# Down projection of a two-layer decoder trunk: weight combinations, residuals and sums of squares all on VectorE, second weight tile in a tile of its own

## The chip, the cores and the metric

One core of one Trainium2 chip runs the whole kernel in one launch. The metric is the device time of the launch in microseconds (us); lower is better. The kernel before takes 2494.03 us (median of 3 runs, 2493.29 to 2494.21).

## What is computed

Two decoder layers on 1024 positions of width 1024, in fp32: a mixer, a SwiGLU feed-forward block and a gated embedding per layer. The change lies in the last product of the feed-forward block, in both layers.

```python
def swiglu(h, w_gate, w_up, w_down):
    return (jax.nn.silu(h @ w_gate) * (h @ w_up)) @ w_down
...
h = h + swiglu(rmsnorm(h, g_ffn[layer]), w_gate[layer], w_up[layer], w_down[layer])
gate = jax.nn.sigmoid(rmsnorm(h, g_ple[layer]) @ w_ple_gate[layer])
h = h + gate * (p[layer] @ w_ple_proj[layer])
```

`w_down` is 2816 x 1024 per layer.

## The kernel before

An fp32 operand is split into a rounded high part and a low rest (`split`, line 145: ScalarE casts the high part, L146, VectorE subtracts it, L147), and each 128x512 product takes three matmuls (`mm3`, lines 189 to 191).

`ffn_down` (line 653) computes the product with `w_down` by Winograd's form of Strassen's scheme on 2x2 blocks: seven products j, in the order 1, 2, 5, 6, 3, 7, 4, instead of eight. Each product has 11 **steps** f = 0 to 10, one per 128 rows of half of `w_down`; step s = 0 to 76 counts through all seven. A step needs one weight tile (128x512) and one activation tile `ra` (128x512, written to DRAM earlier by `ffn_up`), and gives 4 PSUM tiles x 3 = 12 matmuls, 924 in all for a layer. I call the 11 steps of one j a **block**.

The weight tile of a step is made by `left` (line 667). For j = 1, 2, 4 it is a quarter of `w_down` as it is. For the others it is a combination, one add or subtract of 128x512: L673 (j = 5, two tiles read, the sum goes to a kept tile `sd`, one for each f), L677 (j = 6, from `sd` and one tile read), L681 (j = 3, likewise), L684 (j = 7, two tiles read). In the kernel before `tt` (line 659) puts all four on GpSimd (POOL in the profile). Every tile read is a `raw` tile (profile name `rd`), of which there are 6 (`RAW`); so a step of j = 5 or 7 takes two of them.

`run` (line 746) goes through the steps: matmuls of step s, then `prepare(s + 7)`, which reads and combines the weight tile and splits both operands of a step seven ahead. The split tiles are 8 deep. In step f = 8 of a block `before(j)` reads four tiles of the residual and adds the kept partial results `u` or `v` to them (`residual`, L702, POOL). At the end of a block `after(j, ps)` empties the four PSUM tiles: ScalarE copies (j = 1, 5), or VectorE adds (L723), and for j = 6 four adds `v = v + u` on POOL (L733). PSUM tiles come from 6 banks, a block uses 4, so a block's third tile (c = 2) takes the bank that the previous block's first tile (c = 0) held: **matmuls of c = 2 in a block's first step wait for the first add of `after`**. `done` (line 705) scales a finished tile for the next product (L150, L151) and adds its square to a sum `S` (`stat`, L259: POOL, the last of each half on VectorE).

All reads and writes go through one queue, SP. Each engine works through its own queue in order; the framework's scheduler fixes that order when the kernel is built, and it moves instructions ahead of where the source has them. The residual stream's tiles are `hm` (read, line 406) and `hf` (written, line 708).

Of the kernel before, what the change touches and what calls it, by code (L numbers as in the profile page):

```python
# [11 lines left out]
F32 = mybir.dt.float32  # L12
# [4 lines left out]
ALU = mybir.AluOpType  # L17
# [4 lines left out]
P = 128  # L22
T = 1024
D = 1024
KT = D // P
NT = T // P
HT = 512
# [12 lines left out]
RAW = 6  # L40
# [6 lines left out]
class Build:  # L47
# [198 lines left out]
            )  # L246
        return y

    def stat(self, st, n, i, last, src):

        nc = self.nc
        if i == 0:
            st[n] = self.tp.tile([P, HT], F32, tag="S", name=self.name("S"), bufs=2)
            nc.scalar.activation(st[n], src, AF.Square)
        else:
            sq = self.tmp("sq")
            nc.scalar.activation(sq, src, AF.Square)  # L257
            eng = nc.vector if i == last else nc.gpsimd
            eng.tensor_tensor(out=st[n], in0=st[n], in1=sq, op=ALU.add)  # L259

    def tok_scale(self, S, dim, r):
# [63 lines left out]
def trunk(ctx, tc, x, p, positions, g_mix, g_ffn, g_ple, ev_w_in, ev_w_conv, ev_g_v, ev_w_s,  # L325
          ev_b_s, ev_w_out, od_w_in, od_b_gate, od_g_qa, od_g_kva, od_w_q_up, od_w_kv_up, od_g_q,
          od_g_k, od_g_mh, od_w_out, w_gate, w_up, w_down, w_ple_proj, w_ple_gate, out):
    nc = tc.nc
    B = Build(tc)
    x = x[0]  # L330
    out = out[0]
# [316 lines left out]
    half = NFF // 2  # L648
# [4 lines left out]
    def ffn_down(l, act_d, h_d, h2_d, X2, st, normed):  # L653

        steps = [(j, f) for j in (1, 2, 5, 6, 3, 7, 4) for f in range(half)]
        ready, chain, u, v, res = {}, {}, {}, {}, {}
        tt = nc.gpsimd.tensor_tensor

        def part(fh, ch, f):
            t = B.wp.tile([P, HT], F32, tag="raw", name=B.name("rd"), bufs=RAW)
            r = (fh * half + f) * P
            nc.sync.dma_start(t, w_down[l][r : r + P, ch * HT : (ch + 1) * HT])
            return t

        def left(j, f):
            if j in (1, 2, 4):
                return part(j != 1, j == 4, f)
            if j == 5:  # L670
                a, b = part(0, 1, f), part(1, 1, f)
                c = chain[f] = B.slot(32 + f if f < 8 else 35 + f, F32, "sd")
                tt(out=c, in0=a, in1=b, op=ALU.add)  # L673
                return c
            if j == 6:
                a, c = part(0, 0, f), chain[f]
                tt(out=c, in0=c, in1=a, op=ALU.subtract)  # L677
                return c
            if j == 3:
                a = part(1, 0, f)  # L680
                tt(out=a, in0=a, in1=chain[f], op=ALU.subtract)  # L681
                return a
            a, b = part(0, 0, f), part(0, 1, f)
            tt(out=a, in0=a, in1=b, op=ALU.subtract)  # L684
            return a

        def prepare(s):
            j, f = steps[s]
            b = B.slot(RA_SLOTS[s % len(RA_SLOTS)], F32, "ra")
            nc.sync.dma_start(b, act_d[j][f])  # L690
            a = left(j, f)
            wh = B.wp.tile([P, HT], F32R, tag="whi", name=B.name("hd"), bufs=8)
            wl = B.wp.tile([P, HT], F32R, tag="wlo", name=B.name("ld"), bufs=8)
            B.split(wh, wl, a)
            bs = B.slots2(2 * (s % 8), 2 * (s % 8) + 1, "act")
            B.split(bs[0], bs[1], b)
            ready[s] = (wh, wl), bs

        def residual(n, k, plus):
            t = load(h_d[n][k], "res")  # L700
            if plus is not None:
                tt(out=t, in0=t, in1=plus, op=ALU.add)  # L702
            return t

        def done(n, k, t):
            make_ple(l, X2, n, k, t)
            B.stat(st, n, k, KT - 1, t)
            nc.sync.dma_start(h2_d[n][k], t)

        def before(j):  # L710

            for c in range(4):
                if j == 2:
                    res[c] = residual(1, c, u[c])
                elif j == 3:
                    res[c] = residual(0, c, v[c])
                elif j == 7:
                    res[c] = residual(0, c + 4, v[c])
                elif j == 4:
                    res[c] = residual(1, c + 4, u[c])  # L720

        def after(j, ps):
            add = lambda o, a, b: nc.vector.tensor_tensor(out=o, in0=a, in1=b, op=ALU.add)  # L723
            for c in range(4):
                if j == 1:
                    u[c] = B.slot(46 + c, F32, "ud")
                    nc.scalar.copy(u[c], ps[c])
                elif j == 5:
                    v[c] = B.slot(50 + c, F32, "vd")
                    nc.scalar.copy(v[c], ps[c])  # L730
                elif j == 6:
                    add(u[c], ps[c], u[c])
                    tt(out=v[c], in0=v[c], in1=u[c], op=ALU.add)  # L733
                else:
                    if j == 7:
                        add(u[c], ps[c], u[c])
                    add(res[c], ps[c], res[c])
                    n, k = {2: (1, c), 3: (0, c), 7: (0, c + 4), 4: (1, c + 4)}[j]
                    if j == 4:
                        done(n, k, res[c])  # L740
                    else:
                        B.later(c + 1, lambda n=n, k=k, t=res[c]: done(n, k, t))
            if j == 7:
                B.later(4, lambda: normed(0))

        def run():
            for s, (j, f) in enumerate(steps):
                if f == 0:
                    ps = [B.ps("pd") for _ in range(4)]
                if f == half - 3:  # L750
                    before(j)
                a, b = ready.pop(s)
                for c in range(4):
                    w = slice(c * P, (c + 1) * P)
                    B.mm3(ps[c], (a[0][:, w], a[1][:, w]), b, f == 0, f == half - 1)
                B.tick()
                if s + AHEAD < len(steps):
                    prepare(s + AHEAD)
                if f == half - 1:
                    after(j, ps)  # L760
                if s == len(steps) - 4:
                    tok = load_p(l, 0)
            return tok

        return prepare, run
# [187 lines left out]
    for hq in range(2):  # L953
        t = B.tp.tile([P, 4, P], F32, tag="S", name=B.name("wsr"), bufs=2)
        nc.sync.dma_start(t, ev_w_s[0, hq * 4 : hq * 4 + 4].rearrange("h t s -> t h s"))
        nc.gpsimd.affine_select(
            out=t, in_=t, pattern=[[0, 4], [-1, P]], compare_op=ALU.is_ge, fill=0.0, base=0,
# [68 lines left out]
    for pr in range(4):  # L1026
        u = u_unit(pr) if pr else u0
# [12 lines left out]
    for ch in range(4):  # L1040
# [3 lines left out]
        u = B.w_unit(w_in[:, 512 + ch * P : 512 + (ch + 1) * P], KT, P, f"c{ch}", G_MIX)  # L1044
        for n in range(2):
            pc = B.ps(f"pc{ch}")
            B.ws_mm(pc, u, KT, X[n])
            c = B.tmp("cs")
# [3 lines left out]
        u = B.w_unit(w_in[:, 1024 + ch * P : 1024 + (ch + 1) * P], KT, P, f"x{ch}", G_MIX)  # L1052
        ys = []
        for n in range(2):
# [8 lines left out]
            for i in (1, 0):  # L1063
                nc.vector.scalar_tensor_tensor(
                    out=y, in0=z[n][:, i : i + HT], scalar=w[i], in1=y, op0=ALU.mult, op1=ALU.add
# [3 lines left out]
        u = B.w_unit(w_in[:, ch * P : (ch + 1) * P], KT, P, f"b{ch}", G_MIX)  # L1069
# [123 lines left out]
    for i in range(16):  # L1193
# [3 lines left out]
        out=ang, in0=posf.unsqueeze(2).to_broadcast([P, NT, 16]),  # L1197
        in1=freq.unsqueeze(1).to_broadcast([P, NT, 16]), op=ALU.mult,
# [3 lines left out]
        out=turns, in0=ang, scalar1=1.0 / (2 * math.pi), scalar2=ROUND, op0=ALU.mult, op1=ALU.add  # L1202
    )
    nc.vector.tensor_scalar(
        out=turns, in0=turns, scalar1=-ROUND, scalar2=None, op0=ALU.add
    )
    fl = lambda t: t.rearrange("p a b -> p (a b)")
    for c in (TWO_PI_A, TWO_PI_B, TWO_PI_C):
        nc.vector.scalar_tensor_tensor(
            out=fl(ang), in0=fl(turns), scalar=-c, in1=fl(ang), op0=ALU.mult, op1=ALU.add  # L1210
        )
    nc.vector.tensor_scalar(
        out=ang, in0=ang, scalar1=3.1415925, scalar2=-3.1415925, op0=ALU.min, op1=ALU.max
# [5 lines left out]
        out=fl(ang), in0=fl(ang), scalar=-1.0, in1=fl(ang), op0=ALU.mult, op1=ALU.max  # L1219
    )  # L1220
    nc.vector.tensor_scalar(
        out=ang, in0=ang, scalar1=-1.0, scalar2=math.pi / 2, op0=ALU.mult, op1=ALU.add
# [10 lines left out]
        out=qsc[0:NOPE, :], in0=vec[0:NOPE, G_Q : G_Q + 1], scalar1=sc, scalar2=None, op0=ALU.mult  # L1233
# [200 lines left out]
    for tt in range(NT):  # L1434
# [3 lines left out]
        for c in range(2):  # L1438
# [6 lines left out]
            out=q[:, :, 0:NOPE], in0=q[:, :, 0:NOPE],  # L1445
            in1=rn.unsqueeze(2).to_broadcast([P, H, NOPE]), op=ALU.mult,
# [3 lines left out]
            out=qp, in0=q[:, :, NOPE:QK], in1=rp.unsqueeze(2).to_broadcast([P, H, RP]), op=ALU.mult  # L1450
        )
        nc.gpsimd.tensor_tensor(
            out=qp, in0=qp, in1=gqp.unsqueeze(1).to_broadcast([P, H, RP]), op=ALU.mult
# [3 lines left out]
        t = B.tmp("mv")  # L1457
# [23 lines left out]
    for tt in range(NT):  # L1481
# [3 lines left out]
        k = zp.tile([P, H, QK], F32, tag="q", name=B.name("k"), bufs=2)  # L1485
        v = B.tmp("v", (P, H, DV))
        rt = rkv[tt // 4][:, tt % 4 : tt % 4 + 1]
        for c in range(2):
# [10 lines left out]
            out=k[:, :, 0:NOPE], in0=k[:, :, 0:NOPE],  # L1499
            in1=rn.unsqueeze(2).to_broadcast([P, H, NOPE]), op=ALU.mult,  # L1500
# [3 lines left out]
        t = B.tmp("mo")  # L1504
# [25 lines left out]
    for n in range(2):  # L1530
        t = mq_part(0, n, B.ps("mq"))
# [29 lines left out]
    def load_V(pr):  # L1561
# [14 lines left out]
        out=mf, in_=mf, pattern=[[-1, P]], compare_op=ALU.is_ge, fill=NEG, base=0,  # L1576
# [7 lines left out]
        out=mf, in_=mf, pattern=[[1, P]], compare_op=ALU.is_ge, fill=NEG, base=0,  # L1584
# [260 lines left out]
    for i, u in enumerate(units):  # L1845
        h, b = u
# [93 lines left out]
```

## Time and profile before

| | us |
|---|---|
| median of 3 runs | 2494.03 |
| the profiled execution | 2495.41 |
| its span, first to last instruction | 2493.7 |
| TensorE busy (PE) | 2428.1, 97% of the span |
| VectorE busy (DVE) | 1574.7, 63% |
| GpSimd busy (POOL) | 991.7, 40% |
| ScalarE busy (ACT) | 988.2, 40% |
| down stage of layer 0 / of layer 1 (first to last `pd` matmul) | 795.5 to 1015.7 / 2146.7 to 2365.5 |

The profiled execution is 1.7 us longer than its span and 1.4 us longer than the median. In the rows below PE, DVE, ACT and POOL are the four engines that compute, SPq is the queue of reads and writes. Names such as `rd` or `pd` are the program's tiles, with numbers left out; `pd` are the PSUM tiles of the down stage. In square brackets behind an instruction stands how long its engine was idle before it, and what ended that.

### The profile page before, as it was taken

What the parts mean: (1) busy time and instruction counts of PE and PEld (TensorE: products, weight loads), DVE (VectorE), ACT (ScalarE), POOL (GpSimd) and SP (SyncE); (2) the same over time, 40 slices, a digit from 0 to 9 for tenths busy, and PEclk for the clock granted to TensorE, in tenths of its full rate; (3) what the DMA queues carried; (4) which work ended last, traced back from release to release, by engine and by line L of the source; (5) the groups of instructions that cost most, each with busy time, mean ns of one, the idle gap of its engine ahead of it and who ended that gap; (6) DMA issues with size and microseconds to landing.
All of it is one profiled execution on the core that took longest, in us unless ns stands there. A gap on an engine that the chain in (4) does not pass through costs nothing. (4 is left out here: it accounts for less than half of the span.)

```text
span 2493.7 us, 34019 instructions
## 1 busy us (share of the span) xinstructions
PE 2428.1 (97%) x11510; PEld 2004.3 (80%) x11510; DVE 1574.7 (63%) x2879; ACT 988.2 (40%) x1877; POOL 991.7 (40%) x878
## 2 busy tenths in 40 slices
PE   8999998999999998999999999999999999999999
PEld 6878886788888887788888788877788888887877
DVE  6863477545456798776785566557755554697832
ACT  5321344233233545444554455534333232454520
POOL 3452125746553564212321132113556556275400
PEclk9999999999999999999999999999999999999999
DMA  4221443433236857553454843154433233786821
GB/s 149 81 81 51 144 152 96 141 97 110 93 105 208 274 187 258 168 177 95 115 152 124 212 114 104 49 165 123 123 123 114 89 106 106 249 266 192 295 101 39
DMA packets 358686, 350.75 MB, mean 141 GB/s; under 512 B 24011, under 2 KB 249648, under 8 KB 358512
## 3 DMA queue, kind: packets, MB, share of 16 engines
q1 hardware_dynamic: 358016, 348.25, 44.6%
q8 instruction: 90, 1.47, 0.2%
q0 software_dynamic: 464, 0.33, 0.1%
q14 instruction: 84, 0.69, 0.1%
q10 hardware_dynamic: 32, 0.01, 0.0%
HBM read 255.18 MB, written 93.32 MB: 140 GB/s over the span
## 5 line engine op out<-in xcount | busy, mean ns | idle before, releaser
L189 PE MATMUL pd<-acth,hd 128*128 128x512 f32 x616 | 241.9, 393 | 12.3 <-DVE res L723 12.3
L190 PE MATMUL pd<-actl,hd 128*128 128x512 f32 x616 | 241.1, 391 | 0.0
L191 PE MATMUL pd<-acth,ld 128*128 128x512 f32 x616 | 240.9, 391 | 0.0
L259 POOL TENSOR_TENSOR S<-S,sq 128x512 f32<-128x512 f32 x62 | 89.4, 1441 | 255.7 <-ACT sq L257 254.9
L189 PE MATMUL p<-xch,hg 128*128 128x512 f32 x440 | 175.2, 398 | 10.8 <-ACT o L548 8.7
L191 PE MATMUL p<-xch,lg 128*128 128x512 f32 x440 | 174.3, 396 | 0.0
L190 PE MATMUL p<-xcl,hg 128*128 128x512 f32 x440 | 173.9, 395 | 0.0
L189 PE MATMUL p<-xch,hu 128*128 128x512 f32 x440 | 172.9, 393 | 0.0
L191 PE MATMUL p<-xch,lu 128*128 128x512 f32 x440 | 172.9, 393 | 0.0
L190 PE MATMUL p<-xcl,hu 128*128 128x512 f32 x440 | 172.6, 392 | 0.0
L147 DVE TENSOR_TENSOR actl<-ra,acth 128x512 fp32r<-128x512 f32 x154 | 165.2, 1075 | 11.3 <-ACT acth L146 11.1
L189 PEld LDWEIGHTS pd<-acth,hd 128*128 128x128 f32 x616 | 116.6, 189 | 37.5 <-DVE res L723 13.2
L146 ACT CAST hu<-ru 128x512 fp32r<-128x512 f32 x116 | 71.6, 622 | 188.0 <-PE p L190 175.2
L190 PEld LDWEIGHTS pd<-actl,hd 128*128 128x128 f32 x616 | 116.6, 189 | 24.2
L191 PEld LDWEIGHTS pd<-acth,ld 128*128 128x128 f32 x616 | 116.5, 189 | 24.4
L147 DVE TENSOR_TENSOR ld<-rd,hd 128x512 fp32r<-128x512 f32 x110 | 101.6, 923 | 51.3 <-ACT hd L146 51.0
L146 ACT CAST hg<-rg 128x512 fp32r<-128x512 f32 x110 | 68.2, 620 | 158.0 <-PE p L190 131.7
L540 POOL TENSOR_TENSOR act<-act,sg 128x512 f32<-128x512 f32 x60 | 88.6, 1479 | 103.0 <-DVE act L533 102.9
L147 DVE TENSOR_TENSOR lu<-ru,hu 128x512 fp32r<-128x512 f32 x116 | 118.8, 1024 | 15.0 <-ACT hu L146 15.0
L146 ACT CAST hd<-rd 128x512 fp32r<-128x512 f32 x110 | 68.3, 621 | 140.8 <-PE pd L190 61.6
L189 PEld LDWEIGHTS p<-xch,hg 128*128 128x128 f32 x440 | 83.5, 190 | 32.7 <-ACT o L548 9.5
L146 ACT CAST acth<-ra 128x512 fp32r<-128x512 f32 x154 | 94.7, 616 | 26.9 <-DMA ra<-act 22.2
(553 smaller groups left out, 6825.7 us busy)
## 6 DMA issues: line engine op xcount, KB each, us to landing
rd<-in_w_down SPq DMA_DIRECT2D x198, 256.0 KB, 4.1
ra<-act SPq DMA_DIRECT2D x154, 256.0 KB, 3.9
rg<-in_w_gate SPq DMA_DIRECT2D x100, 256.0 KB, 3.3
ru<-in_w_up SPq DMA_DIRECT2D x100, 256.0 KB, 2.9
act<-act SPq DMA_DIRECT2D x88, 256.0 KB, 2.0
act<-at SPq DMA_DIRECT2D x66, 256.0 KB, 2.0
rpg<-in_w_ple_gate SPq DMA_DIRECT2D x48, 256.0 KB, 3.0
rwo<-in_ev_w_out SPq DMA_DIRECT2D x32, 256.0 KB, 2.8
```

The lines of the kernel that those rows point to most:

```text
L146: self.nc.scalar.copy(hi, src)
L147: (eng or self.nc.vector).tensor_tensor(out=lo, in0=src, in1=hi.bitcast(F32), op=ALU.subtract)
L189: mm(ps, a[0], b[0], start=first, stop=False, skip_group_check=more)
L190: mm(ps, a[0], b[1], start=False, stop=False, skip_group_check=more)
L191: mm(ps, a[1], b[0], start=False, stop=last, skip_group_check=more)
L259: eng.tensor_tensor(out=st[n], in0=st[n], in1=sq, op=ALU.add)
L540: (nc.vector if last else nc.gpsimd).tensor_tensor(out=t, in0=t, in1=sg[d["i"], key], op=ALU.mult)
```

## The change

- `tt` becomes VectorE: the 44 combinations of a stage (L673, L677, L681, L684), the 16 residual adds (L702) and the 4 adds `v = v + u` (L733).
- `done` passes VectorE to `stat`: the 12 adds of squares of a stage that POOL had (L259).
- For j = 5 and j = 7 the second weight tile is read straight into the `sd` tile of that f, not into a `raw` tile. For j = 5 the combination is then made in place.
- The four residual tiles of a block are no longer read and added together in step 8, but one each in steps 5, 6, 8 and 9.

```diff
-    def stat(self, st, n, i, last, src):
+    def stat(self, st, n, i, last, src, eng=None):
...
-            eng = nc.vector if i == last else nc.gpsimd
+            eng = eng or (nc.vector if i == last else nc.gpsimd)
             eng.tensor_tensor(out=st[n], in0=st[n], in1=sq, op=ALU.add)
...
-        tt = nc.gpsimd.tensor_tensor
-
-        def part(fh, ch, f):
-            t = B.wp.tile([P, HT], F32, tag="raw", name=B.name("rd"), bufs=RAW)
+        tt = nc.vector.tensor_tensor
+
+        def part(fh, ch, f, t=None):
+            if t is None:
+                t = B.wp.tile([P, HT], F32, tag="raw", name=B.name("rd"), bufs=RAW)
...
+            spot = lambda: B.slot(32 + f if f < 8 else 35 + f, F32, "sd")
             if j == 5:
-                a, b = part(0, 1, f), part(1, 1, f)
-                c = chain[f] = B.slot(32 + f if f < 8 else 35 + f, F32, "sd")
-                tt(out=c, in0=a, in1=b, op=ALU.add)
+                a, c = part(0, 1, f), part(1, 1, f, spot())
+                chain[f] = c
+                tt(out=c, in0=a, in1=c, op=ALU.add)
                 return c
...
-            a, b = part(0, 0, f), part(0, 1, f)
+            a, b = part(0, 0, f), part(0, 1, f, spot())
             tt(out=a, in0=a, in1=b, op=ALU.subtract)
             return a
...
-            B.stat(st, n, k, KT - 1, t)
+            B.stat(st, n, k, KT - 1, t, nc.vector)
...
-                if f == half - 3:
-                    before(j)
+                if f in (5, 6, 8, 9):
+                    before(j, (5, 6, 8, 9).index(f))
```

The number of instructions and of transfers stays the same. VectorE's queue grows by 152 instructions (76 a stage) and POOL's shrinks by as many. What that does to the queues is seen at two places of layer 0; the numbers behind the names tell tiles apart.

The first place is VectorE's queue just ahead of the four adds that empty the PSUM tiles of product 3. Before, `ld` and `actl` are the low parts of the weight and the activation tile, two rows for a step:

```order
L147 TENSOR_TENSOR ld_8289<-rd_8283,hd_8288 128x512
L147 TENSOR_TENSOR actl_8293<-ra_8281,acth_8292 128x512
L147 TENSOR_TENSOR ld_8316<-rd_8310,hd_8315 128x512
L147 TENSOR_TENSOR actl_8320<-ra_8308,acth_8319 128x512
L723 TENSOR_TENSOR res_8230<-pd_8018,res_8230 128x512
L723 TENSOR_TENSOR res_8233<-pd_8019,res_8233 128x512
```

The same place in the changed kernel (L686 is the old L684, L724 the old L723):

```order
L147 TENSOR_TENSOR ld_8218<-rd_8212,hd_8217 128x512
L147 TENSOR_TENSOR actl_8222<-ra_8210,acth_8221 128x512
L686 TENSOR_TENSOR rd_8376<-rd_8376,sd_8378 128x512
L147 TENSOR_TENSOR ld_8248<-rd_8242,hd_8247 128x512
L147 TENSOR_TENSOR actl_8252<-ra_8240,acth_8251 128x512
L686 TENSOR_TENSOR rd_8411<-rd_8411,sd_8413 128x512
L147 TENSOR_TENSOR ld_8278<-rd_8272,hd_8277 128x512
L147 TENSOR_TENSOR actl_8282<-ra_8270,acth_8281 128x512
L686 TENSOR_TENSOR rd_8446<-rd_8446,sd_8448 128x512
L147 TENSOR_TENSOR ld_8305<-rd_8299,hd_8304 128x512
L147 TENSOR_TENSOR actl_8309<-ra_8297,acth_8308 128x512
L724 TENSOR_TENSOR res_8138<-pd_8007,res_8138 128x512
```

The combinations of product 7 now stand in VectorE's own queue ahead of those adds, four steps ahead of the `ld` of the same step (`rd_8376`, f = 8, stands ahead of `ld_8248`, f = 4).

The second place is the SP queue where it reads product 7's weights. Before, each step has two reads into `raw` tiles beside its `ra`:

```order
L664 DMA rd_8256<-in_w_down 128x512
L690 DMA ra_8281<-act_3164 128x512
L664 DMA rd_8258<-in_w_down 128x512
L664 DMA rd_8283<-in_w_down 128x512
L690 DMA ra_8308<-act_3165 128x512
L664 DMA rd_8285<-in_w_down 128x512
L664 DMA rd_8310<-in_w_down 128x512
```

In the changed kernel it has one there:

```order
L665 DMA rd_8341<-in_w_down 128x512
L692 DMA ra_8339<-act_3166 128x512
L665 DMA rd_8376<-in_w_down 128x512
L692 DMA ra_8374<-act_3167 128x512
L665 DMA rd_8411<-in_w_down 128x512
L692 DMA ra_8409<-act_3168 128x512
L665 DMA rd_8446<-in_w_down 128x512
```

The other half of product 7's weights, the `sd` tiles, is read some 15 steps earlier for f = 0 to 5 (beside the `ra` of products 6 and 3):

```order
L665 DMA sd_8127<-in_w_down 128x512
L692 DMA ra_7761<-act_3156 128x512
L665 DMA sd_8157<-in_w_down 128x512
L665 DMA sd_8187<-in_w_down 128x512
L665 DMA sd_8214<-in_w_down 128x512
L692 DMA ra_7786<-act_3157 128x512
L665 DMA sd_8244<-in_w_down 128x512
```

So the reads of product 7 are spread over a longer stretch of the queue, and half of them no longer wait for a `raw` tile.

## Rows read from the trace of the kernel before

**Rows 1.** The page's section 1: busy us and share of the span, instructions.
```profile
PE 2428.1 (97%) x11510; PEld 2004.3 (80%) x11510; DVE 1574.7 (63%) x2879; ACT 988.2 (40%) x1877; POOL 991.7 (40%) x878
```

**Rows 2.** Waits of PE, whole span: engine, line, releaser: us in total, times, longest.
```profile
PE pd L189 <- DVE res L723: 12.3, 2, 6.2
```

**Rows 3.** Timeline of PE, layer 0: start us, us, instruction, [idle before, releaser].
```profile
944.77 0.39 PE L190 MATMUL pd<-actl,hd 128*128 128x512 f32 x1
...
946.36 0.39 PE L191 MATMUL pd<-acth,ld 128*128 128x512 f32 x1
952.99 0.79 PE L189 MATMUL pd<-acth,hd 128*128 128x512 f32 x1 [6.24 <-DVE res L723]
...
956.81 0.40 PE L189 MATMUL pd<-acth,hd 128*128 128x512 f32 x1
```

**Rows 4.** Timeline of PE, the same place in layer 1 (12 matmuls apart).
```profile
2297.44 0.39 PE L191 MATMUL pd<-acth,ld 128*128 128x512 f32 x1
...
2308.54 0.39 PE L191 MATMUL pd<-acth,ld 128*128 128x512 f32 x1
```

**Rows 5.** Windows, layer 0: us, busy (instructions) by engine, PE clock, DMA share, GB/s.
```profile
795.50:1016.00 220.50, 213.72 (x938) 175.89 (x937) 182.85 (x199) 102.25 (x181) 121.15 (x78) 0.98 0.71 237
931.00:946.00 15.00, 15.00 (x68) 12.43 (x67) 7.38 (x11) 4.57 (x8) 5.84 (x6) 1.00 0.52 179
955.00:956.00 1.00, 1.00 (x4) 0.81 (x3) 1.00 (x3) 1.00 (x3) 0.26 (x1) 0.50 0.88 283
961.00:976.00 15.00, 15.00 (x68) 12.43 (x67) 14.17 (x14) 6.79 (x13) 10.13 (x7) 1.00 0.98 340
```

**Rows 6.** Timeline of DVE, the end of the wait.
```profile
951.04 0.69 DVE L147 TENSOR_TENSOR ld<-rd,hd 128x512 fp32r<-128x512 f32 x1 [1.84 <-ACT hd L146]
...
952.25 1.28 DVE L723 TENSOR_TENSOR res<-pd,res 128x512 f32<-128x512 f32 x2
```

**Rows 7.** Timeline of POOL, from the end of product 6 to the wait.
```profile
925.98 5.15 POOL L702 TENSOR_TENSOR res<-res,vd 128x512 f32<-128x512 f32 x3
...
945.85 1.37 POOL L684 TENSOR_TENSOR rd<-rd,rd 128x512 f32<-128x512 f32 x1 [1.15 <-DMA rd<-in_w_down]
949.09 1.26 POOL L684 TENSOR_TENSOR rd<-rd,rd 128x512 f32<-128x512 f32 x1 [1.88 <-DMA rd<-in_w_down]
```

**Rows 8.** Timeline of SP (its reads), the same stretch.
```profile
948.14 2.57 SPq L664 DMA_DIRECT2D rd<-in_w_down  x2
```

**Rows 9.** Timeline of all engines, product 6: DVE with POOL at work, then without.
```profile
882.26 10.27 POOL L681 TENSOR_TENSOR rd<-rd,sd 128x512 f32<-128x512 f32 x6
...
889.60 1.78 DVE L147 TENSOR_TENSOR actl<-ra,acth 128x512 fp32r<-128x512 f32 x1
...
891.30 1.78 DVE L147 TENSOR_TENSOR ld<-sd,hd 128x512 fp32r<-128x512 f32 x1
...
894.21 0.68 DVE L147 TENSOR_TENSOR actl<-ra,acth 128x512 fp32r<-128x512 f32 x1
...
894.81 0.68 DVE L147 TENSOR_TENSOR ld<-sd,hd 128x512 fp32r<-128x512 f32 x1
```

**Rows 10.** Groups by line, layer 0's down stage: xcount, busy us, mean ns, idle before.
```profile
L147 DVE TENSOR_TENSOR actl<-ra,acth 128x512 fp32r<-128x512 f32 x69 | 78.9, 1144 | 2.8 <-ACT acth L146 2.8
...
L684 POOL TENSOR_TENSOR rd<-rd,rd 128x512 f32<-128x512 f32 x11 | 15.9, 1444 | 17.9 <-DMA rd<-in_w_down 12.9 <-DVE actl L147 5.0
```

**Rows 11.** The tile `rd`: its 198 reads from issue to landing.
```profile
DMA to landing us min/median/max: 2.5/4.1/6.9
```

**Rows 12.** Timeline of PE, just after layer 0's down stage.
```profile
1021.83 0.39 PE L191 MATMUL ppg<-xph,lpg 128*128 128x512 f32 x1
1023.93 1.08 PE L266 MATMUL rs<-ones_f,S 128*128 128x1 f32 x8 [1.72 <-DVE pTl L147]
1024.87 0.78 PE L189 MATMUL ppj<-pTh,hpj 128*128 128x512 f32 x1
...
1028.36 0.39 PE L191 MATMUL ppg<-xph,lpg 128*128 128x512 f32 x1
```

More of the change, by code (lines that the diff above doesn't have):

```diff
@@ L706, in done, with before @@
             make_ple(l, X2, n, k, t)
-            B.stat(st, n, k, KT - 1, t)
+            B.stat(st, n, k, KT - 1, t, nc.vector)
             nc.sync.dma_start(h2_d[n][k], t)
[L710 to L720, printed above, removed]
+        def before(j, c):
+            if j == 2:
+                res[c] = residual(1, c, u[c])
+            elif j == 3:
+                res[c] = residual(0, c, v[c])
+            elif j == 7:
+                res[c] = residual(0, c + 4, v[c])
+            elif j == 4:
+                res[c] = residual(1, c + 4, u[c])
         def after(j, ps):
```

## The prediction

> **What bounds the kernel now.** I read the page first: TensorE is busy 97% of the span [rows 1], so time can only come from the places where it stands still or runs slowly. The list of TensorE's waits comes next: in the down stages there is one large kind, matmuls of `pd` that wait for the VectorE add at L723, 12.3 us in two waits [rows 2], one a layer. The timeline shows the wait: matmuls start 0.227 us apart (seven of them from 944.77 to 946.36), then the next starts at 952.99 instead of 946.59 [rows 3]. It is the third tile (c = 2) of product 7's first step, which needs the bank that the first add after product 3 frees. And the wait costs more than its length. After it TensorE has a granted clock of 0.50, which is 1.2 of 2.4 GHz [rows 5], for eight matmuls, and only then 0.23 us a matmul again. The price in layer 0: from 946.36 to 956.81 there are ten matmuls, 10.45 us where 10 x 0.227 = 2.27 would do, so 8.18 us [rows 3]. In layer 1 twelve matmuls take 2297.44 to 2308.54, 11.10 instead of 2.73, so 8.37 us [rows 4]. **Both together: 16.55 us.**
>
> Why is that add late? VectorE begins it at 952.25, though the PSUM tile was complete before 946. Ahead of it in the queue stands a `ld` that waited for ScalarE's cast `hd` [rows 6], and the cast waits for POOL's combination, which waits for a read of `rd` [rows 7]. That read was issued late: the two reads of a step span 2.57 us, since the second waits until a `raw` tile comes free [rows 8]. It isn't the memory that is slow: in the stretch before the wait the DMA engines are 0.52 busy, and 0.98 when the tiles flow again [rows 5]. So the chain is: six `raw` tiles, two a step, make three steps of prefetch; POOL's combinations of product 7 run 3.2 us apart (945.85, 949.09 [rows 7]) where TensorE takes 12 x 0.227 = 2.73 us a step; and they began late, since residual adds had stood ahead of them in POOL's queue (three of them 5.15 us [rows 7]).
>
> A last view: how fast VectorE is. While POOL works through six combinations VectorE's starts lie 1.70 us apart (889.60, 891.30); when POOL rests they lie 0.60 apart (894.21, 894.81) [rows 9]. Over the stage its `actl` take 1144 ns on average [rows 10] against the 680 of the undisturbed ones.
>
> **The change, part by part.** *Adds moved to VectorE.* 44 combinations, 16 residual adds, 4 adds of `v` and 12 of squares make 76 a stage. POOL loses 76 x 1.44 us = 109 us (the mean of L684 [rows 10] for all) and then has next to nothing to do there, so VectorE's adds go at 0.60 us [rows 9]. Its load: (199 + 76) x 0.60 = 165 us of the 220.5 us stage, where it is busy 182.85 us now [rows 5]. The price lies beside TensorE's work as long as every block's share fits. A block lasts 11 x 2.73 = 30.0 us. Counted in the changed queue from one set of PSUM adds to the next, product 2's block holds 43 instructions, product 5's 44, product 6's 27, product 3's 45, product 7's 37; at 0.60 that is 25.8, 26.4, 16.2, 27.0 and 22.2 us. All fit; product 3's is the tightest. I cost the moved adds at nothing; if the cover goes, the price is what the PSUM adds come late.
>
> *Waits that VectorE inherits.* A combination waits for its read, and now `ld`, `actl` and the PSUM adds queue behind it. In product 3's block the last three combinations (f = 8, 9, 10 of product 7) are read into `raw` tiles freed by the `ld` that stands 6, 5 and 5 instructions ahead, 3.6, 3.0 and 3.0 us. A read lands 2.5 to 6.9 us after its issue, median 4.1 [rows 11]. At the median the waits are 0.5 + 1.1 + 1.1 = 2.7 us, and 27.0 + 2.7 = 29.7. Allowed are 30.0 + 1.4 (c = 2 comes six matmuls into the block) - 0.7 (the add itself) = 30.7 us. So no stall, with 1 us to spare; at 2.5 nothing waits, at 6.9 it is 7.4 us too late. I take the median, because in that block each step reads one `rd` and one `ra`, no heavier than the average of the rows. The Trainium skill (SBUF — State Buffer, section "The DMA setup-cost knee") gives a transfer a fixed 2 us and 436 GB/s beyond, an estimate of 2.6 us for 256 KB: by it nothing would wait here and 3.7 us would be spare. The 4.1 of this trace decides, so I keep the risk.
>
> *Second weight tile in `sd`.* Products 5 and 7 take one `raw` tile a step instead of two: six steps of prefetch instead of three. Half of product 7's reads stand up to 15 steps earlier in SP's queue. The number of bytes stays. This removes the late reads of product 7 at their source: the 16.55 us go. What is late next in that block is `ld` of step 61, which waits for a split tile that TensorE frees, and that is on time by construction.
>
> *Residual tiles one by one.* Sixteen adds at 0.60 us, in the ledger above; their reads stand early in SP's queue. Nothing on the path.
>
> *End of the stage.* In layer 0 TensorE waits once more for VectorE (`pTl`, and the sum `S` ahead of it): 1021.83 to 1023.93 is 2.10 instead of 0.23 us, and eight slow matmuls follow, 1024.87 to 1028.36, 3.49 instead of 1.82 [rows 12]: 3.5 us. The changed queue has three more `S` adds there (1.8 us) but no pitch of 1.70 us. Between nothing gained and 3.5 us a layer I take 2.5 us for layer 0, where the rows show the loss, and none for layer 1, of whose end I have no such row.
>
> **Sum:** 16.55 + 2.5 = 19.05 us. The profiled execution would be 2495.41 - 19.05 = 2476.36; the median is 1.38 below it, so **2475.0 us**.
>
> **The rivals.** *A smaller wait comes back.* If the three reads land in 5.4 us, 3 x 1.3 = 3.9 us more waiting against 1 us to spare makes the add 2.9 us late, and with the slow matmuls behind it (1.8 us, from rows 3: 10.45 - 6.40 - 2.27) 4.7 us a stage: 2475 + 9.4 = 2484 us. For it: the reads' spread [rows 11]. Against it: the DMA engines are half idle there [rows 5].
>
> *No change.* The wait is the memory's: three tiles a step, 0.98 of the DMA engines at 340 GB/s [rows 5], whatever their buffers. Then the 6.2 us stay: 2494 us. Against it speaks 0.52 just before.
>
> *Slower: VectorE's queue is blocked by reads.* POOL could wait for reads without harm; VectorE can't. At the longest landing, 6.9 us, the adds after product 3 are 7.4 us late, with the slow matmuls 9.2; and the same at the end of product 2, where all eleven combinations of product 5 stand ahead of the adds: 2 x 18.4 = 37 us, 2475 + 37 = 2512 us. One such place alone (2493) is still no loss; it decides from the second on. Against it: reads that long are the tail of the rows.
>
> *VectorE becomes the bound.* Taken at face value, 182.85 us of busy time [rows 5] plus 76 x 0.68 = 52 is 234.5 us in a stage of 220.5: 14 us more a stage, 2494 + 28 = 2522 us. The Trainium skill (Perfetto Trace Analysis, section "Optimizing Scalar/DVE Operations") says that with VectorE saturated, work may be better given to ScalarE or even GpSimd, the reverse of this change, and adds that between GpSimd and VectorE it might not help. By the first half of that rule this rival would be the forecast. Rows 9 speak against it: the busy time is stretched by POOL itself.
>
> **How the numbers follow.** Both waits gone, no new one: 0.64, at 2475 us (2470 to 2480 by the stage ends: 0 to 7 us gained there). A smaller wait: 0.17, 2481 to 2489. No change: 0.07. VectorE's queue blocked: 0.08; VectorE the bound: 0.04. A measurement of this kernel tells 0.2%, 5 us, from no change. So faster 0.81, same 0.07, slower 0.12. The range holds the first two cases: 2470 to 2489 us.
>
> **What would show it.** Right: the list of TensorE's waits has no `pd <- res` above 1 us; POOL is nearly idle in both stages; `actl` and `ld` of VectorE average about 0.7 us instead of 1.1; VectorE is busy 165 to 190 us a stage. Wrong: a wait of `pd` at the start of product 5 or 7 with VectorE idle before a combination, "until DMA `rd`"; or VectorE without idle time through a whole block.

## The result and the profile after

The changed kernel takes 2475.6 us (median of 4 runs, 2473.82 to 2477.41), the kernel before 2493.66 beside it; the ratio is 0.9926 with a 95% interval of 0.9912 to 0.9940, so it is faster by 0.6 to 0.9%. The forecast was 2475.0. The number came out; the reason given for its largest term did not, as the experiments show.

The profiled execution took 2476.73 us, its span is 2475.0, 18.7 less than before. Busy time over the whole span, to be held against [rows 1]:

```profile
PE 2423.9 (98%) x11510; PEld 2001.0 (81%) x11510; DVE 1544.6 (62%) x3031; ACT 987.2 (40%) x1877; POOL 750.9 (30%) x726
```

VectorE has 152 instructions more and is busy 30 us *less*; GpSimd is busy 241 us less. The list of TensorE's waits, which had 12.3 us of `pd` [rows 2], has no `pd` any more. In layer 0, from 790 to 1020 us, this is all of it:

```profile
PE p L189 <- DVE act L533: 0.5, 1, 0.5
PE Rb L299 <- POOL dg L288: 0.4, 1, 0.4
```

The window of layer 0's down stage answers to the first line of [rows 5], the groups by line (layer 0's stage) to [rows 10], the reads of `rd` to [rows 11]:

```profile
795.50:1008.00 212.50, 211.97 (x941) 175.09 (x940) 165.70 (x274) 102.09 (x182) 7.73 (x5) 1.00 0.74 243
```

```profile
L147 DVE TENSOR_TENSOR actl<-ra,acth 128x512 fp32r<-128x512 f32 x69 | 49.4, 716 | 3.1 <-ACT acth L146 3.1
...
L686 DVE TENSOR_TENSOR rd<-rd,sd 128x512 f32<-128x512 f32 x11 | 7.5, 686 | 0.5 <-DMA rd<-in_w_down 0.5
...
L675 DVE TENSOR_TENSOR sd<-rd,sd 128x512 f32<-128x512 f32 x11 | 7.3, 688 | 4.8 <-DMA rd<-in_w_down 4.8
```

```profile
DMA to landing us min/median/max: 2.5/4.0/6.4
```

TensorE is without a gap in the stage. VectorE does 274 instructions in 165.70 us, where it needed 182.85 us for 199: `actl` takes 716 ns instead of 1144, a combination 686 where GpSimd took 1444. GpSimd works 7.73 us instead of 121.15. The reads land as late as before.

The place of the old 6.24 us wait [rows 3, 6], first TensorE, then VectorE:

```profile
946.33 0.39 PE L191 MATMUL pd<-acth,ld 128*128 128x512 f32 x1
946.56 0.39 PE L189 MATMUL pd<-acth,hd 128*128 128x512 f32 x1
```

```profile
942.26 0.69 DVE L686 TENSOR_TENSOR rd<-rd,sd 128x512 f32<-128x512 f32 x1 [0.54 <-DMA rd<-in_w_down]
...
944.36 2.48 DVE L724 TENSOR_TENSOR res<-pd,res 128x512 f32<-128x512 f32 x4
```

The third tile of product 7 starts in step (946.56, 0.23 after the matmul before it). Before, the waiting matmul started 0.74 us after the add that it waited for (952.25 to 952.99 in [rows 3, 6]); by that the bank is free at 945.10 here, some 1.5 us early. At the end of product 2 there is less to spare: the add starts at 855.70, which makes 856.44, and the matmul that needs its bank starts at 856.80, 0.4 us later.

Where the 18.7 us of the span came from. A stage runs here from the start of its first to the start of its last `pd` matmul; the second row goes on to the 200th matmul of TensorE after that:

| stretch | before | after | gain |
|---|---|---|---|
| down stage, layer 0 | 220.01 | 211.70 | 8.31 |
| from there to the 200th matmul | 47.87 | 44.74 | 3.13 |
| down stage, layer 1 | 218.60 | 210.19 | 8.41 |
| from its last `pd` to the end of the span | 128.44 | 129.03 | -0.59 |
| all the rest | 1878.8 | 1879.3 | -0.6 |

The wait at the end of layer 0's stage [rows 12] is gone too: the eight `rs` follow without a wait, and the matmuls after them are not slow.

```profile
1014.31 0.97 PE L266 MATMUL rs<-ones_f,S 128*128 128x1 f32 x8
1015.15 0.48 PE L190 MATMUL ppj<-pTl,hpj 128*128 128x512 f32 x1
```

In layer 1 the end of the stage gained nothing. TensorE waits there before and after the change, at the same transposes. First before, then after:

```profile
2374.49 0.95 PE L787 MATMUL ptr<-ident,ptok 128*128 128x128 f32 x4 [0.93 <-DVE pTl L147]
```

```profile
2352.78 0.50 PE L189 MATMUL ppj<-wjh,pTh 128*128 128x512 f32 x1 [0.52 <-ACT pTh L146]
...
2355.37 0.66 PE L788 MATMUL ptr<-ident,ptok 128*128 128x128 f32 x2 [1.41 <-DMA ptok<-in_p]
```

`ptok` are rows of the embedding input. Their second half is read only after the stage: the read is issued 5.0 us after the last `pd` matmul in both kernels (2370.22 and 2350.94) and takes 4.1 us before and 4.3 after. Before, VectorE's `pTl` was ready at the same moment as the read, at 2374.36; now it is ready earlier, and the read alone holds TensorE.

### The profile page after: what moved, and what is told of

Same layout as the page of the kernel before. It is cut to its first block, busy times and chain, and to the rows that moved or that the text cites. A ratio compares the mean times of both kernels' runs of the same rounds, so it can differ in the third digit from the quotient of the medians.

```text
span 2475.0 us, 33946 instructions
## 1 busy us (share of the span) xinstructions
PE 2423.9 (98%) x11510; PEld 2001.0 (81%) x11510; DVE 1544.6 (62%) x3031; ACT 987.2 (40%) x1877; POOL 750.9 (30%) x726
## 4 chain that ended last, share of the span: by engine, by line
PE 50%; DVE 4%; issue 2%; DMA 1%; POOL 1%; ACT 1%; SPq 0%; POOLq 0%; DVEq 0%; ACTq 0%
PE p L189 5%; PE p L190 5%; PE p L191 5%; PE pd L189 3%; PE pd L190 3%; PE pd L191 3%; PE O L1829 2%; PE ppg L191 2%; PE ppg L190 2%; PE ppg L189 2%; PE PT L1871 1%; PE po L189 1%; PE po L190 1%; PE po L191 1%; PE S L1771 1%
## 5 line engine op out<-in xcount | busy, mean ns | idle before, releaser
L259 POOL TENSOR_TENSOR S<-S,sq 128x512 f32<-128x512 f32 x38 | 51.7, 1362 | 220.5 <-ACT sq L257 220.5
L147 DVE TENSOR_TENSOR actl<-ra,acth 128x512 fp32r<-128x512 f32 x154 | 109.7, 714 | 13.4 <-ACT acth L146 13.2
L147 DVE TENSOR_TENSOR ld<-rd,hd 128x512 fp32r<-128x512 f32 x110 | 77.0, 700 | 46.0 <-ACT hd L146 46.0
L288 POOL TENSOR_TENSOR dg<-ident,rl 128x512 fp32r<-128x512 f32 x10 | 13.7, 1370 | 289.7 <-DVE rl L284 265.9
```

The costliest lines, as they stand in the source:

```text
L147: (eng or self.nc.vector).tensor_tensor(out=lo, in0=src, in1=hi.bitcast(F32), op=ALU.subtract)
L288: (nc.vector, nc.gpsimd)[i].tensor_tensor(out=d, in0=self.ident.unsqueeze(1).to_broadcast([P, 4, P]), in1=x.unsqueeze(2).to_broadcast([P, ...
```

## Experiments

The change has two parts that could each have removed the wait: the second weight tile in `sd` (theory A: the reads were late for want of `raw` tiles) and the adds on VectorE (theory B: GpSimd and VectorE slow each other down). The first four kernels take the parts apart.

### The tile alone

```diff
 # the kernel before, and:
-                a, b = part(0, 1, f), part(1, 1, f)
-                c = chain[f] = B.slot(32 + f if f < 8 else 35 + f, F32, "sd")
-                tt(out=c, in0=a, in1=b, op=ALU.add)
+                a, c = part(0, 1, f), part(1, 1, f, spot())
+                chain[f] = c
+                tt(out=c, in0=a, in1=c, op=ALU.add)
...
-            a, b = part(0, 0, f), part(0, 1, f)
+            a, b = part(0, 0, f), part(0, 1, f, spot())
```

> The kernel before with one part of the change: the second weight tile of a step of products 5 and 7 is read into its sd tile. Combinations, residual adds and squares stay on GpSimd, residuals at f = 8. Theory A (late reads): product 7's combinations were late because six raw tiles, two a step, held back the reads. Then the pd <- res waits go on both layers (below 1 us), the time falls by the 16.6 us priced for them to about 2477 us, and VectorE's pitch stays stretched (actl above 1.0 us on average, VectorE busy about 180 us in layer 0's stage). Theory B (contention): GpSimd's adds, each stretched and stretching VectorE's, are what makes the chain late. Then a pd <- res wait of 3 us or more stays in each layer and the time stays above 2485 us.

Measured: 2506.94 us (2497.20 to 2510.96), ratio 1.0047 (1.0029 to 1.0064): *slower* than before. The waits of TensorE for the PSUM adds:

```profile
PE pd L189 <- DVE res L725: 16.3, 4, 5.5
```

At the start of product 7 the wait is 3.13 us in layer 0 instead of 6.24, and 2.70 in layer 1. A new one stands at the start of product 5, 5.49 and 5.00 us. What happened ahead of it (in layer 0 the matmul waits until 862.67) is seen in the window from 833 to 862, first of the kernel before, then of this one:

```profile
833.00:862.00 29.00, 29.00 (x130) 24.01 (x129) 24.87 (x25) 14.80 (x27) 17.62 (x13) 1.00 0.93 311
```

```profile
833.00:862.00 29.00, 24.18 (x107) 19.71 (x105) 29.00 (x19) 9.14 (x16) 28.64 (x18) 0.95 0.77 254
```

and in the timelines of GpSimd and of VectorE:

```profile
834.30 8.55 POOL L675 TENSOR_TENSOR sd<-rd,sd 128x512 f32<-128x512 f32 x5
843.21 8.14 POOL L675 TENSOR_TENSOR sd<-rd,sd 128x512 f32<-128x512 f32 x5 [0.36 <-DMA ra<-act]
851.32 11.83 POOL L679 TENSOR_TENSOR sd<-sd,rd 128x512 f32<-128x512 f32 x7
```

```profile
836.51 1.79 DVE L147 TENSOR_TENSOR actl<-ra,acth 128x512 fp32r<-128x512 f32 x1
838.22 1.78 DVE L147 TENSOR_TENSOR ld<-sd,hd 128x512 fp32r<-128x512 f32 x1
...
860.27 1.74 DVE L147 TENSOR_TENSOR actl<-ra,acth 128x512 fp32r<-128x512 f32 x1
861.94 2.47 DVE L725 TENSOR_TENSOR res<-pd,res 128x512 f32<-128x512 f32 x4
864.33 0.74 DVE L151 SCALAR_TENSOR_TENSOR xpl<-res,vec,xph 128x512 fp32r<-128x512 f32 x1
```

The earlier reads let GpSimd run almost without a pause (28.64 of 29 us), and as long as it does, VectorE's `ld` and `actl` start 1.70 us apart; it is never idle in the window and does 19 instructions where it did 25. The PSUM adds, which came at 855.62 in the kernel before, come at 861.94. In the kernel before GpSimd's waits for its reads had given VectorE time at full pace. So theory A, on which my sum's largest term rested, doesn't hold by itself: without the late reads the wait at product 7 is half as long, and a longer one than was saved stands at product 5. The stages of the profiled execution (2500.38 us) are 4.1 and 2.5 us longer than before; the median is 6.6 us longer than that execution, and what the longer ones lose no trace shows.

### The adds on VectorE alone

```diff
 # the changed kernel, and:
-            spot = lambda: B.slot(32 + f if f < 8 else 35 + f, F32, "sd")
...
-                a, c = part(0, 1, f), part(1, 1, f, spot())
-                chain[f] = c
-                tt(out=c, in0=a, in1=c, op=ALU.add)
+                a, b = part(0, 1, f), part(1, 1, f)
+                c = chain[f] = B.slot(32 + f if f < 8 else 35 + f, F32, "sd")
+                tt(out=c, in0=a, in1=b, op=ALU.add)
...
-            a, b = part(0, 0, f), part(0, 1, f, spot())
+            a, b = part(0, 0, f), part(0, 1, f)
```

> The changed kernel without the tile: combinations, residual adds and squares on VectorE and residuals one by one, but both weight tiles of a step of products 5 and 7 in raw tiles. Theory A (late reads): the reads of product 7 come late again, and now VectorE itself waits for them, with the ld, the actl and the PSUM adds behind it; a pd <- res wait at the start of product 7 comes back, 3 us or more a layer with slow matmuls behind it, and the time is 2485 to 2500 us. Theory B (contention): at a pitch of 0.60 us the raw tiles come free soon enough; no pd wait above 1 us, and 2475 to 2478 us.

Measured: 2478.32 us (2476.63 to 2479.44), ratio 0.9939 (0.9927 to 0.9951). Nearly all of the gain is there without the tile: theory B on the time, 0.3 us above its range. No wait above 1 us at the start of product 7; but a smaller one in each layer at the start of product 5:

```profile
PE pd L189 <- DVE res L723: 4.9, 2, 3.0
```

VectorE's timeline ahead of it in layer 0, five of the six waits for a read from 838 to 859:

```profile
838.49 0.69 DVE L674 TENSOR_TENSOR sd<-rd,rd 128x512 f32<-128x512 f32 x1 [1.55 <-DMA rd<-in_w_down]
...
845.49 0.69 DVE L674 TENSOR_TENSOR sd<-rd,rd 128x512 f32<-128x512 f32 x1 [2.35 <-DMA rd<-in_w_down]
847.98 0.69 DVE L674 TENSOR_TENSOR sd<-rd,rd 128x512 f32<-128x512 f32 x1 [0.59 <-DMA rd<-in_w_down]
...
854.91 0.69 DVE L674 TENSOR_TENSOR sd<-rd,rd 128x512 f32<-128x512 f32 x1 [1.18 <-DMA rd<-in_w_down]
857.65 0.69 DVE L678 TENSOR_TENSOR sd<-sd,rd 128x512 f32<-128x512 f32 x1 [2.05 <-DMA rd<-in_w_down]
...
859.46 1.88 DVE L723 TENSOR_TENSOR res<-pd,res 128x512 f32<-128x512 f32 x3
```

This is the prediction's rival "VectorE's queue is blocked by reads", at the place that it names second, at the end of product 2. What the tile does in the change is to keep it away: 218.20 us for layer 0's stage here, 211.70 with the tile; 212.76 and 210.19 in layer 1. By these profiles the tile is worth 9.1 us on top of the move, by the medians 2.7 us. Of the 9.1 us 4.9 are the two waits, the rest slow matmuls behind them. The medians' intervals (0.9927 to 0.9951 here, 0.9912 to 0.9940 with the tile) overlap, and the stretch between the two stages, from the 200th matmul to layer 1's first `pd`, was 4.7 us shorter in this profile than in that of the changed kernel, without any edit there. That stretch scatters: 1078.7 us here, 1079.4 and 1083.4 in two kernels further down that leave it alone too (squares back, GpSimd adds), 1083.4 in the changed kernel. So the two waits are the tile's worth that is shown, and the time doesn't measure it.

### Residual tiles bunched

```diff
-                if f in (5, 6, 8, 9):
-                    before(j, (5, 6, 8, 9).index(f))
+                if f == half - 3:
+                    for c in range(4):
+                        before(j, c)
```

> The changed kernel with the four residual tiles of a block read and added together at f = 8, as in the kernel before. My reasoning in the prediction: their adds are in the ledger anyway and nothing stands on the path, so 2475.6 us within 2 us, no pd wait above 1 us. Rival: the four adds and reads in a row just ahead of the end of a block use up the 0.4 us that the changed kernel's trace shows to spare after product 2 (add ends 856.4, needed 856.8) and the 1.5 us after product 3; then a pd <- res wait of 1 to 3 us with 1.8 us of slow matmuls in one or both places of each layer, 2480 to 2490 us.

Measured: 2473.19 us (2471.50 to 2477.91), ratio 0.9927 (0.9912 to 0.9942); stages of 211.74 and 210.18 us, no `pd` wait. The median is 0.4 us below the range expected, the ratio that of the changed kernel. This part of the change moves nothing that can be measured, as the prediction had it.

### Squares back on GpSimd

```diff
-            B.stat(st, n, k, KT - 1, t, nc.vector)
+            B.stat(st, n, k, KT - 1, t)
```

> The changed kernel with the 12 adds of squares of a stage back on GpSimd, nothing else. My term for the stage's end: the 3.5 us lost in layer 0's end before (a wait of S and pTl and eight slow matmuls) came from VectorE's stretched pitch; with GpSimd's adds of squares back, only they overlap VectorE's work at block ends. If the squares alone make that loss, it returns: a wait of rs or ptr near the end of layer 0's stage, and 2478 to 2480 us. Rival: it was the combinations' contention and backlog that made it; then 2475.6 us within 1.5 us and no wait at layer 0's end. VectorE adds that overlap a GpSimd add should show 1.2 us or more instead of 0.68.

Measured: 2476.92 us (2473.26 to 2478.62), ratio 0.9931 (0.9918 to 0.9943). The median lies in the rival's range, and the runs spread over both; the trace has the first expectation's wait. At the end of layer 0's stage, GpSimd, VectorE and TensorE:

```profile
1009.01 4.71 POOL L259 TENSOR_TENSOR S<-S,sq 128x512 f32<-128x512 f32 x3 [12.29 <-ACT sq L257]
```

```profile
1010.79 3.48 DVE L151 SCALAR_TENSOR_TENSOR xpl<-res,vec,xph 128x512 fp32r<-128x512 f32 x2
1014.20 0.68 DVE L259 TENSOR_TENSOR S<-S,sq 128x512 f32<-128x512 f32 x1
```

```profile
1015.53 1.05 PE L266 MATMUL rs<-ones_f,S 128*128 128x1 f32 x8 [1.72 <-DVE pTl L147]
```

The wait of [rows 12] is back, 1.72 us as it was there. The way to the 200th matmul is 46.81 us: of the 3.13 us that the change won there, the squares alone bring back 2.07. Three GpSimd adds stand beside the `xpl`, which take 1.7 us each instead of 0.74; that part of the prediction's term is shown. A smaller loss came in layer 1's stage (211.69 us), a wait of 1.18 us at the start of product 5, the place with 0.4 us to spare.

### GpSimd adds that nobody needs

If contention decides, it must be possible to put the loss back into the changed kernel while its reads and its combinations stay as they are.

```diff
             B.split(wh, wl, a)
+            if 11 <= s < 66:
+                if s == 11:
+                    scr[0] = B.slot(31, F32, "scr")
+                nc.gpsimd.tensor_tensor(out=scr[0], in0=wh.bitcast(F32), in1=wh.bitcast(F32), op=ALU.add)
```

> The changed kernel with 55 more GpSimd adds of 128x512 a stage, one for each step of products 2, 5, 6, 3 and 7; each reads the high part of the step's weight tile and writes a tile that nobody reads. Theory C (contention decides, formed after the tile alone made the kernel slower): while a GpSimd add runs, VectorE's adds of two SBUF operands go at 1.70 us instead of 0.60, so each of the 55 costs VectorE about 1.1 us: 275 x 0.60 + 55 x 1.1 = 225 us a stage, more than the 212 us that the stage has. Then pd <- res waits come back, each stage takes at least 225 us, and the time is 2500 us or more. Rival (the late reads decided, contention lies in VectorE's slack): VectorE is busy more but no pd wait over 1 us, 2475 to 2480 us.

Measured: 2508.55 us (2506.74 to 2512.79), ratio 1.0066 (1.0051 to 1.0082): the 55 idle adds a stage cost 33 us, more than the whole change had won. The stages take 228.97 and 227.85 us. Waits of TensorE over the whole span, and groups of VectorE in layer 0's stage:

```profile
PE pd L189 <- DVE res L729: 24.2, 4, 6.3
```

```profile
L147 DVE TENSOR_TENSOR actl<-ra,acth 128x512 fp32r<-128x512 f32 x69 | 66.9, 969 | 2.7 <-ACT acth L146 2.7
...
L680 DVE TENSOR_TENSOR sd<-sd,rd 128x512 f32<-128x512 f32 x11 | 9.8, 909 | 0.0
...
L729 DVE TENSOR_TENSOR res<-pd,res 128x512 f32<-128x512 f32 x15 | 9.5, 678 | 0.0
```

In the timeline one GpSimd add makes one VectorE instruction last 1.53 us instead of 0.68, or costs 0.85 us; I had put 1.1. The window of the stage, for the line of the changed kernel above:

```profile
795.50:1025.50 230.00, 216.82 (x941) 177.81 (x940) 205.20 (x274) 102.18 (x181) 78.27 (x60) 0.97 0.70 225
```

VectorE is busy 39.5 us more than 165.70, or 0.72 for each of the 55 adds: 48 of its instructions in the stage are stretched to about 1.5 us. Its 205.20 us are still less than the 212 of the stage, so theory C's sum over the stage isn't what brings the waits. An estimate by the prediction's blocks does: eleven adds at 0.85 are 9.4 us, which makes 35.2 us for product 2's block and 36.4 for product 3's, where 30.7 are allowed, and 25.6 for product 6's. The four waits are at the starts of products 5 and 7, right behind these two blocks, in both layers, where the tile-alone run has them. (Product 7's block comes to 31.6, and no wait follows it.)

One rival has to be ruled out: the adds read `hd`, a tile of which there are 8, so ScalarE's next casts could be late for their sake, and the profile does name them as what those casts waited for:

```profile
844.92 0.62 ACT L146 CAST hd<-sd 128x512 fp32r<-128x512 f32 x1 [1.58 <-POOL scr L701]
```

```profile
844.45 0.39 PE L190 MATMUL pd<-actl,hd 128*128 128x512 f32 x1
```

But this cast starts 0.08 us after the end (844.84) of the last matmul that reads the tile it overwrites, and so do all but one of the 27 casts of layer 0's stage with that name behind them; in the changed kernel the lag is 0.04 to 0.08 us too. So TensorE paces the casts, and the loss is VectorE's stretched pitch: theory C's cause holds. It is enough for a loss of this size; how the old 6.24 us divide between it and GpSimd's own slower chain, no run shows.

### GpSimd copies that nobody needs

```diff
-                nc.gpsimd.tensor_tensor(out=scr[0], in0=wh.bitcast(F32), in1=wh.bitcast(F32), op=ALU.add)
+                nc.gpsimd.tensor_copy(scr[0], wh.bitcast(F32))
```

> As the run with 55 GpSimd adds, but each of the 55 is a copy (one operand read) of the same tile to the same place. If any GpSimd access to these tiles stretches VectorE, the pitch beside a copy is 1.7 us too and the time lies within 5 us of the run with adds. If it takes an add's second operand, VectorE keeps 0.60 us beside the copies, no pd wait over 1 us, and the time is 2475 to 2480 us.

Measured: 2482.32 us (2480.34 to 2487.99), ratio 0.9958 (0.9941 to 0.9975), stages of 215.94 and 213.72 us. Neither expectation. The waits are back at the same four places, but shorter, and VectorE's timeline has instructions of 1.10 us beside the copies:

```profile
PE pd L189 <- DVE res L729: 6.7, 4, 2.5
```

```profile
843.05 1.10 DVE L147 TENSOR_TENSOR ld<-sd,hd 128x512 fp32r<-128x512 f32 x1
844.07 0.68 DVE L147 TENSOR_TENSOR actl<-ra,acth 128x512 fp32r<-128x512 f32 x1
```

So a copy costs 0.42 us where an add costs 0.85. The price depends on what GpSimd does, not on the mere fact that it works. Whether it is the second operand or only that a copy is over sooner (the shortest take 0.61 and 1.04 us), these runs don't separate.

### `ptok` of layer 1 read earlier

```diff
                 if s == len(steps) - 4:
                     tok = load_p(l, 0)
+                    if l == 1:
+                        early_tok[1] = load_p(l, 1, (44, 45))
...
-            pT[n] = make_pT(load_p(l, n) if n else tok, [32 + 4 * n + i for i in range(4)])
+            pT[n] = make_pT(early_tok[1] if n else tok, [32 + 4 * n + i for i in range(4)])
```

> The changed kernel with the second half of the embedding rows of layer 1 (ptok) read four steps before the stage's end, beside the first half, into two tiles that product 7 has left free; before, they were read after the stage, for want of a tile. In the changed kernel TensorE waits 1.41 us for them and then runs slowly for a few matmuls. Expected: no ptr <- ptok wait in layer 1, the way from its last pd matmul to the end of the span falls from 129.0 us by 2 to 3.5 us; the median 2472 to 2474 us. Rival: the wait is followed by another (pTh, the split of the transposed rows) and less than 1 us is won.

Measured: 2471.11 us (2469.87 to 2471.79), ratio 0.9913 (0.9898 to 0.9928). The `ptok` wait is gone; TensorE's one wait left there is

```profile
PE ppj L189 <- ACT pTh L146: 1.0, 1, 1.0
```

and the way from the last `pd` to the end is 126.4 us instead of 129.0. The 2.6 us are in the range expected, but that way scatters: it took 126.9 to 127.5 us in four kernels above that make no edit there (adds alone, residuals bunched, GpSimd adds, GpSimd copies). Against those the gain is about 1 us. The median is 0.9 us below the range expected, and its interval overlaps that of the changed kernel. That the wait goes is shown, how much it wins is not.

### The same move in the stage ahead

In the changed kernel's `ffn_up` GpSimd still makes the weight combinations. Its timeline and ScalarE's and TensorE's there:

```profile
385.56 5.89 POOL L179 TENSOR_TENSOR su<-ru,ru 128x512 f32<-128x512 f32 x1 [9.84 <-DVE lg L147]
```

```profile
394.07 0.62 ACT L146 CAST hu<-su 128x512 fp32r<-128x512 f32 x1 [5.33 <-POOL su L180]
```

```profile
398.73 0.80 PE L189 MATMUL p<-xch,hg 128*128 128x512 f32 x1 [5.72 <-ACT o L548]
```

```diff
-        tt = self.nc.gpsimd.tensor_tensor
+        tt = self.nc.vector.tensor_tensor
         raw = lambda: self.wp.tile([P, 4, P], F32, tag="raw", name=self.name(f"s{name}"), bufs=RAW)
...
-                        nc.gpsimd.tensor_tensor(out=r[3], in0=r[2], in1=r[6], op=ALU.subtract)
+                        nc.vector.tensor_tensor(out=r[3], in0=r[2], in1=r[6], op=ALU.subtract)
```

> The changed kernel with the same move in the stage ahead, ffn_up: its 88 combinations of weight tiles a layer (L179 to L181, L510) go from GpSimd to VectorE. In the changed kernel one of these adds on GpSimd takes 5.89 us (from 385.56) while VectorE works without a gap, the cast hu waits 5.33 us for it, and TensorE waits 5.72 us behind that cast, with slow matmuls after it; the same in layer 1 (2.9 us). If the lesson carries, these waits go or shrink: 2460 to 2470 us. Rival: VectorE has no gap there from 371 to 390, and more work for it makes TensorE wait longer: 2476 to 2490 us.

Measured: 2467.53 us (2465.38 to 2469.47), ratio 0.9896 (0.9880 to 0.9913). The four combinations that took GpSimd 9.8 us (385.56 to 395.4) take 3.7 us on VectorE (386.50 to 390.2), the last of them being

```profile
389.51 0.69 DVE L510 TENSOR_TENSOR ru<-ru,su 128x512 f32<-128x512 f32 x1
```

and in layer 0 the waits of 5.7 and 2.9 us become 2.9 and 2.2. The stages of `ffn_up`, from first to last `p` matmul, fall from 440.6 to 438.1 and from 440.0 to 436.9 us: 5.6 of the 8.1 us by which the medians differ.

### Both additions

The two edits above in one kernel.

> The changed kernel with both additions that won by themselves: ptok of layer 1 read four steps earlier, and the weight combinations of ffn_up on VectorE. They lie in different stages, so they should add: 4.5 us (2475.6 to 2471.1) and 8.1 us (2475.6 to 2467.5) give 2463.0 us, 2461 to 2466. Rival: part of one is slack that the other already uses, 2467 us or more.

Measured: 2465.30 us (2463.40 to 2466.88), ratio 0.9886 (0.9869 to 0.9902) against the kernel before, an interval below that of the changed kernel (0.9912 to 0.9940). They add, less some 2 us, inside the range expected.

## Why the prediction was right, and which step of it was not

- **The term of 16.55 us.** Measured 8.31 + 8.41 = 16.72. What stood still, what it cost in slow matmuls and that it would go were right.
- **The cause under that term failed; that the number held owes much to luck.** The prediction wrote of the second tile: "This removes the late reads of product 7 at their source: the 16.55 us go", and costed the moved adds "at nothing". The tile alone halved the wait at product 7, made a new one and gave 2506.94 us; the moved adds alone gave 2478.32. What carried the gain is the row that I used only to price VectorE's load [rows 9]: 1.70 us with GpSimd at work, 0.60 without. I read the chain at product 7 back from the wait to the reads and stopped there; I didn't ask what VectorE would do once GpSimd no longer paused for them. As the change makes both parts together, the sum came out all the same.
- **The ledger by blocks.** 165 us a stage was measured as 165.70. Product 3's block was not the tightest: 1.5 us were to spare there (1 was forecast), 0.4 us after product 2. There the combinations of product 5 waited 4.8 us for their reads (the L675 line above), which the sum left out: 25.8 + 4.8 = 30.6 of the 30.7 us allowed. The reads that I took to cost 2.7 us in product 3's block cost 0.54: the last three (issued at 933.28, 935.71 and 938.43) landed 2.7, 2.7 and 3.7 us after their issue instead of 4.1, and VectorE, ahead of its casts by then, waited 0.82 us twice for `hd`, which gave them time.
- **The rivals.** "VectorE's queue is blocked by reads" is real, and the run without the tile shows it at product 5 with 3.0 us; with the tile it doesn't come up. "VectorE becomes the bound" had the sign right for a kernel in which GpSimd goes on working (2508.55 us with the idle adds) and was wrong for this one, since the work moved leaves GpSimd with 7.73 us. The section of the Trainium skill that the prediction cites for it (Perfetto Trace Analysis, "Optimizing Scalar/DVE Operations") would have work taken off a saturated VectorE and given to ScalarE or GpSimd, and doubts the latter; the doubt is what these runs bear out: with the tile in both, and the bunched residuals without effect, the same 76 adds a stage make 2506.94 us on GpSimd and 2475.6 on VectorE.
- **The stage's end.** In layer 0 3.13 us instead of the 2.5 taken; in layer 1 a loss of 0.6 instead of nothing, where the read of `ptok` comes no earlier than before; other kernels with nothing changed there scatter by more. The two errors cancel, by luck.
- **What would show it.** The `pd <- res` waits gone, GpSimd nearly idle, `actl` at 0.72 us and VectorE busy 165.70 us a stage: all as written.

## To carry to other kernels

Before giving GpSimd tile adds because VectorE looks busy, find in the trace a stretch in which GpSimd rests and compare VectorE's pitch: here 0.60 against 1.70 us, so that 76 adds more cost VectorE no time at all. A late read that makes the slower engine pause can be what keeps the other one on time, as in the kernel before: take the waits out one by one in thought and ask who runs into whom next. And when adds that wait for reads move into a queue with work behind them, give the reads their own tiles, or the wait moves with them.

## Not expected of the hardware

- A GpSimd add of 128x512 fp32 costs VectorE 0.85 us and a copy 0.42 us when they come one a step (1.53 and 1.10 us instead of 0.68). With GpSimd at work without a pause, VectorE's `ld` and `actl` come 1.70 us apart.
- Adds that read a PSUM tile keep their pace: `res<-pd,res` took 678 ns on average in the run with the idle adds, and in the tile-alone run the four from 861.94 go at 0.60 us though GpSimd's series lasts until 863.15. The Trainium skill (SBUF — State Buffer, section "Who interferes with whom") states such a rule: a VectorE instruction with two SBUF inputs contends with a GpSimd instruction that reads SBUF, one with at most one SBUF input does not, outside VectorE's 2-port modes. These rows agree.
- It can go the other way: in `ffn_up` of the changed kernel VectorE goes on at 0.60 us from 385.41 to 390.2, and the GpSimd add that began at 385.56 takes 5.89 us, where the three after it take 1.26 to 1.29. The Trainium skill (SBUF — State Buffer, section "SBUF: two separate sides") says that whichever of the two starts first has the shared ports for its whole instruction, and the other is blocked; here GpSimd stayed behind for some eight VectorE instructions, so this row goes beyond the rule. What decides which of the two is held up for long, no run here shows.
